# Moving two prefetched weight forms behind one subtraction, and naming the PSUM banks of a second pass, in a hybrid encoder layer

## The chip, the core and the metric

The kernel runs on one core of a Trainium2 chip. The metric is device time in microseconds (us), the median of several executions. The core has a matrix engine (TensorE, PE in the profile, with its weight loads listed apart as PEld), a vector engine (VectorE, DVE), a scalar engine (ScalarE, ACT), GpSimd (POOL) and a queue that issues DMAs (SyncE, SP). Products land in PSUM, which here is used as eight banks of 128 partitions x 512 float32. Everything else lives in SBUF.

## The reference

One layer of a bidirectional encoder on x of shape (1, 512, 1024), all float32. A token mixer (retention plus a gated spatial unit) comes first, and then the part that the change touches, a convolutional gated MLP with 2816 hidden columns per half:

```python
def _conv_gated_mlp(h, w_up, conv_w, conv_b, w_down):
    hid = h @ w_up                                   # (512, 1024) @ (1024, 5632)
    hid = depthwise_conv_of_width_3(hid) + conv_b    # along the sequence
    a, b = jnp.split(hid, 2, axis=-1)
    return (jax.nn.gelu(a) * b) @ w_down             # (512, 2816) @ (2816, 1024)

h2 = _rmsnorm(x, g_pre_ffn)
x = x + _rmsnorm(_conv_gated_mlp(h2, ...), g_post_ffn)
```

## The kernel before

**Arithmetic.** Every float32 operand is split into a high and a low part (line 85: `copy(hi, src)` on ACT, then `tensor_sub(lo, src, hi)` on DVE, which is line 87 in the profile), and each product is three matrix instructions: high by high, high by low, low by high. Two-by-two block products are done with seven block products in place of eight (Winograd's form of Strassen's scheme), so weights and activations are also needed as sums and differences, called forms.

**Up product.** The 44 weight blocks of the up product make 22 tiles of a (gate half, value half) pair. Tiles 4 to 19 are taken in eight *couples* (line 40). In a couple the first tile's two blocks go through class `Pair` as seven form products of 12 matrix instructions of 256 columns each, and the second tile's two blocks go through `up_block` as plain products of 48 each, so a couple has 7 x 12 + 2 x 48 = 180 matrix instructions. Their order (lines 1016 to 1020) is: `part1` (four products: with weight forms B11, B21, T1, T2), the first `up_block`, `part2` (the third product into bank 0, with T3), the first half of the second `up_block`, `part3` (products with T4 into bank 0 and B22 into bank 2), the second half of the second `up_block`.

In `part2` the product with T3 is copied out of bank 0 by ACT (line 700) and then subtracted from what stands in bank 2 by DVE (line 701). The first product of `part3` writes bank 0 again, so it needs the copy of line 700. The second writes bank 2, so it needs the subtraction of line 701; it is followed by the subtraction of line 713.

**Weights.** `units` (lines 94 to 118) lists all weight units in the order of their use: in a couple B11, B21, T1, T2, a block, T3, T4, B22, a block. A form has size 1, a block size 2. `w_get` (line 208) hands out the next unit and, before it does, makes later ones as long as the sizes of those made and not yet handed out, the one handed out included, stay within a limit: 9 for a form, 10 for a block. Making a unit (`w_form`, `w_block`, `w_down`) issues its DMA on SP, its sums, its high part on ACT and its low part on DVE. For T1 that is two sums on DVE (lines 166 and 167), one on GpSimd (line 168, which makes T2), and the split. T4 is one sum on GpSimd (line 170) and the split. The raw weights live in 4 buffers and the split ones in 9 slots; a slot is free again when the matrix engine is done with what was in it.

An engine runs its instructions in the order in which they stand in its queue. That order comes from the order of the lines, rearranged by a scheduler that works with modelled times; `tc.issue_after(ins)` ties every instruction of its block that runs on the engine of `ins` to a place behind `ins`.

**Down product.** It runs in two passes over the halves of the output columns. In each pass `products` is called for nine j with 42 matrix instructions each (seven products M1, M2, M3, M5, M6, M7, M4, in this order, of six each), every product into a bank of its own over all j; `add_whole` adds the rows that are not in pairs. Behind the last j of pass one the results are combined out of PSUM by ACT and DVE (`steps`, lines 1092 to 1098), and at the same time pass two starts to fill banks again. In pass two each product takes a bank from the pool (`m[n] = ps()`, line 1046) when j is 0, in the order in which the banks were let go.

Of the kernel before, what the change touches and what calls it, by code (L numbers as in the profile page):

```python
# [28 lines left out]
LOOK = 4  # L29
# [19 lines left out]
def tile_block(ctx: ExitStack, tc, xT, x, wall, par, cs, wsp, bsp, gpost, gpre, gffn, out):  # L49
# [7 lines left out]
    def nm(s):  # L57
        uid[0] += 1
        return f"{s}_{uid[0]}"

    def blk(dt=F32, n="blk", shape=(P, S)):
        return sb.tile(list(shape), dt, tag="blk", bufs=NBLK, name=nm(n))

    def tmp(n="tmp", shape=(P, S)):
        return sb.tile(list(shape), F32, tag="tmp", bufs=6, name=nm(n))
# [7 lines left out]
    def ps(shape=(P, S)):  # L73
        return pp.tile(list(shape), F32, tag="ps", name=nm("ps"))
# [4 lines left out]
    def copy(o, i):  # L79
        nc.scalar.activation(out=o, in_=i, func=AF.Copy)  # L80
# [13 lines left out]
    units = []  # L94
    i = 0
    while i < NW:
# [7 lines left out]
        elif i == UP0 + 2 * COUPLES[0][0]:  # L104
# [3 lines left out]
            i = UP0 + 2 * COUPLES[-1][1] + 2  # L108
# [10 lines left out]
    w_ready, w_pos, w_held, w_raw = {}, [0, 0], [0], {}  # L119
# [79 lines left out]
    def w_size(u):  # L199
        return 2 if u[0] in ("blk", "q", "t") else 1  # L200

    def w_next():
        u = units[w_pos[1]]
        w_ready[w_pos[1]] = w_unit(u)
        w_pos[1] += 1
        return w_size(u)

    def w_get(look=LOOK):

        i = w_pos[0]  # L210
        w_pos[0] += 1
        room = 2 * look + (2 if w_size(units[i]) == 2 else 0)
        n = sum(w_size(u) for u in units[i : w_pos[1]])
        while w_pos[1] < len(units) and (w_pos[1] <= i or n + w_size(units[w_pos[1]]) <= max(room, 9 if look == LOOK else 0)):
            n += w_next()
        return w_ready.pop(i)

# [50 lines left out]
    for k in range(KD):  # L268
        xt = load_x(k)
        xts.append(xt)  # L270
        if k:
            x_low(k, xt)
        if k == 2:
            copy(hold[:, 0:16], as32(xl[1])[:, 0:16])
        wh, wl = w_get(1 if k < 4 else LOOK)
        if k == 0:
            x_low(k, xt)
            for half in range(2):
                for a, b in ((wh, xh), (wl, xh), (wh, xl)):
                    for m in range(4 * half, 4 * half + 4):  # L280
                        nc.tensor.matmul(
                            qk[m], a[:, m * P : (m + 1) * P], b[0], start=a is wh and b is xh, stop=False
                        )
            continue
        if k > 1 and (k - 2) % 4 < 2:
            x_scaled(k - 2, xts[k - 2])
        for m in range(8):
            c = slice(m * P, (m + 1) * P)
            mm3(qk[m], wh[:, c], wl[:, c], xh[k], xl[k], False, k == KD - 1)

    T0, T1 = slice(0, 256), slice(256, 512)
# [53 lines left out]
    v = nc.vector  # L345
# [125 lines left out]
    def t_group():  # L471

        acc = [ps() for _ in range(NT)]
        for kp in range(4):
            wh, wl = w_get()
            for t in range(NT):
                c = slice(t * P, (t + 1) * P)
                for kk in range(2):
                    k = 2 * kp + kk
                    f = slice(kk * S, (kk + 1) * S)  # L480
                    nc.tensor.matmul(acc[t], xh[k][:, c], wh[:, f], start=k == 0, stop=False)  # L481
                    nc.tensor.matmul(acc[t], xh[k][:, c], wl[:, f], start=False, stop=False)  # L482
                    nc.tensor.matmul(acc[t], xl[k][:, c], wh[:, f], start=False, stop=k == KD - 1)  # L483
            yield acc
# [158 lines left out]
    def f_block(ah, al, n, between=None):  # L643

        wh, wl = w_get()
        o = ps()
        for k in range(n):
            if between and k == n // 2:
                between()
            c = slice(k * P, (k + 1) * P)  # L650
            mm3(o, wh[:, c], wl[:, c], ah[k], al[k], k == 0, k == n - 1)
        return o
# [4 lines left out]
    class Pair:  # L657
# [38 lines left out]

        def part2(self):
            c0, c1 = self.t
            o = self.product(0, self.s("S3"), False)
            copy(c1[:, T1], o)  # L700
            v.tensor_sub(c1[:, T1], self.b[2][:, T0], c1[:, T1])  # L701
            self.w = w_get(), w_get()

        def part3(self):
            c0, c1 = self.t
# [202 lines left out]
    def h2_sums(i):  # L908

        a0, b0, a1, b1 = h2r[0][i], h2r[0][i + 2], h2r[1][i], h2r[1][i + 2]  # L910
        v.tensor_sub(b1, a1, b1)
        v.tensor_sub(a1, a0, a1)
        v.tensor_sub(a0, b1, a0)
        v.tensor_add(b0, b0, a0)
        for n, t in zip(("S1", "S2", "S3", "S4"), (b1, a0, a1, b0)):
            h2_parts(n, i, t)

    def h2_block(w, o, q):
        wh, wl = w
        for k in range(KD):  # L920
            c = slice(k * P, (k + 1) * P)
            mm3(o[:, q], wh[:, c], wl[:, c], *h2(k, q), k == 0, k == KD - 1)

    def up_block(between=None):
        w, o = w_get(), ps()
        h2_block(w, o, T0)
        if between:
            between()
        h2_block(w, o, T1)
        return o  # L930
# [73 lines left out]
    def tile_done(i, o):  # L1004
        gated(*(conv(t, 2 * i + s_) for s_, t in enumerate(o)))
        if i < COUPLES[-1][1]:
            if i in (7, 11, 13, 17):
                down_forms(len(dforms))
        elif len(dforms) < EAGER:
            down_forms(len(dforms))  # L1010

    couples = dict(COUPLES)
    i = 0
    while i < NF:
        if i in couples:
            p = Pair(None, lambda: tmp("c"), h2, h2forms)
            p.part1()
            o = [up_block()]
            p.part2()
            o.append(up_block(p.part3))  # L1020
            tile_done(i, p.t)
            tile_done(i + 1, o)
            i += 2
        else:
            o = []
            for e in (2 * i, 2 * i + 1):
                o.append(early_o[e] if e < EARLY else up_block())
            if i < 2:
                h2_sums(i)
                w_next()  # L1030
            tile_done(i, o)
            i += 1
# [5 lines left out]
    M1, M2, M3, M5, M6, M7, M4, M8 = range(8)  # L1038
    whole = []

    def products(m, j, steps={}):
        for n, (unit, at, act) in enumerate(UNITS):
            if n in (0, 3):
                wh, wl = w_get()
            if j == 0:
                m[n] = ps()
            f = slice(at * 256, (at + 1) * 256)
            ah, al = dforms[j][act]
            for t in range(2):
                c = slice(t * P, (t + 1) * P)  # L1050
                o = m[n][:, t * 256 : (t + 1) * 256]
                for i, (a_, w_) in enumerate(((ah, wh), (ah, wl), (al, wh))):
                    nc.tensor.matmul(  # L1053
                        o, a_[:, c], w_[:, f], start=j == t == i == 0,
                        stop=j == DP - 1 and i == 2 and n not in (M2, M3, M4), skip_group_check=True,
                    )
            steps.get(n, lambda: None)()
# [18 lines left out]
    m = {}  # L1076
    m[M8] = ps()
    late = list(range(EAGER, DP))
    c11, c12, c21, c22 = c4 = [blk(n="c") for _ in range(4)]
    e1, e3, uu, yy = tmp("e1"), tmp("e3"), tmp("uu"), tmp("yy")  # L1080

    def after6():
        v.tensor_add(uu, m[M6], e1)
        v.tensor_sub(c12, m[M5], uu)
        v.tensor_add(c12, c12, e3)

    def after7():
        v.tensor_add(e1, m[M7], uu)
        v.tensor_sub(yy, m[M5], e1)  # L1089
        v.tensor_add(c22, c22, yy)  # L1090

    steps = {
        M1: lambda: copy(e1, m[M1]),
        M2: lambda: v.tensor_add(c11, m[M2], e1),
        M3: lambda: copy(e3, m[M3]),
        M6: after6, M7: after7,
        M4: lambda: v.tensor_add(c21, m[M4], e1),
    }
    for j in range(DP):
        if j < WHOLE:  # L1100
            whole.append(two_parts(gp[2 * DP + j]))
        if j % 2 and late:
            down_forms(late.pop(0))
        products(m, j, steps if j == DP - 1 else {})
        if j in (3, 5):
            w = w_get()
            for t in range(NT):
                add_whole(m, t, j // 2 - 1, w, j == 5)
            if j == 5:
                copy(c22, m[M8])  # L1110
# [12 lines left out]
        v.tensor_add(qn[t][:, 0:1], qn[t][:, 2:3], qn[t][:, 3:4])  # L1123


    m = {}
    e1, uu, xx, yy = (blk(n="e") for _ in range(4))

    def after6():
# [3 lines left out]
    def after7():  # L1133
        v.tensor_add(uu, m[M7], uu)
        v.tensor_sub(yy, m[M5], uu)

    steps = {M1: lambda: copy(e1, m[M1]), M6: after6, M7: after7}
    for j in range(DP):
        products(m, j, steps if j == DP - 1 else {})
        if 1 < j < 2 + NT:  # L1140
            first_share(j - 2)
    ww = [w_get(), w_get()]
    m[M8] = ps()

    def rows(t, sc, z, xt, some=(0, 1, 2)):

# [16 lines left out]
    for t in (0, 2, 1, 3):  # L1163
        last = t == NT - 1
# [152 lines left out]
```

## Time and profile before

| | us |
|---|---|
| runs, median (lowest to highest) | 829.89 (827.95 to 831.93) |
| the profiled execution's own time | 832.1 |
| its span, first to last instruction | 830.3 |
| PE busy, share of the span | 819.6, 99% |
| DVE busy | 659.3, 79% |
| ACT busy | 430.9, 52% |
| GpSimd busy | 104.4, 13% |

In the profiled execution the couples run from 520.8 to 683.8 us, the last plain blocks of the up product until 709.5 us, pass one of the down product until 765.2 us and pass two until 822 us. A row of the timeline gives the start, the duration, the engine, the line, the operation, the tiles written and read, the shape, and in brackets how long the engine had stood idle before and what ended that. A row of the table by stretches gives, for each engine, busy time and in brackets the number of instructions that lie in the stretch wholly or in part. Matrix instructions overlap in the records (one lasts 0.28 us and the next starts 0.11 to 0.12 us after it), so the distance of their starts tells the pace and not their busy time.

### The profile page before, as it was taken

To read this page: it belongs to the slowest core of one execution; us is meant where nothing else is said; L and a number is where in the kernel's file an instruction comes from. 1 tells how busy PE (TensorE), PEld (TensorE's weight loads), DVE (VectorE), ACT (ScalarE), POOL (GpSimd) and SP (SyncE) were. 2 spreads that over 40 slices of the span, in tenths; PEclk is the share of its full clock that TensorE was granted. 3 is DMA by queue.
4 is the path that set the end of the run, shared out by engine and by line. 5 is a ranking of instruction groups with operands and counts; after the bars stand their busy time and mean duration, and the time that the engine had idled before them with its cause. 6 is when DMAs were issued, how large, how long until landed. Compare 5 with 4: busy or idle time off the path is not lost. (4 is left out here: it accounts for less than half of the span.)

```text
span 830.3 us, 14356 instructions
## 1 busy us (share of the span) xinstructions
PE 819.6 (99%) x5728; PEld 760.9 (92%) x5728; DVE 659.3 (79%) x1076; ACT 430.9 (52%) x733; POOL 104.4 (13%) x108
## 2 busy tenths in 40 slices
PE   9999999999999999999999999999999999999996
PEld 7888888888899999999988899999999999999995
DVE  7489898877897777767765679679899789997956
ACT  6635445546665444444444456456566566644532
POOL 0010000102221111133221201111111100000002
PEclk9999999999999999999999999999999999999999
DMA  8733222213233333233459121333323341243344
GB/s 279 258 115 104 75 77 77 76 52 99 69 102 126 102 102 93 87 100 102 121 178 349 64 67 37 105 104 99 116 91 101 110 147 50 77 141 103 115 128 127
DMA packets 29251, 93.84 MB, mean 113 GB/s; under 512 B 3392, under 2 KB 4032, under 8 KB 29184
## 3 DMA queue, kind: packets, MB, share of 16 engines
q1 hardware_dynamic: 26784, 86.58, 32.6%
q0 software_dynamic: 1968, 6.03, 2.3%
q8 instruction: 45, 0.74, 0.4%
q10 hardware_dynamic: 432, 0.30, 0.1%
q14 instruction: 22, 0.18, 0.1%
HBM read 88.19 MB, written 4.72 MB: 112 GB/s over the span
## 5 line engine op out<-in xcount | busy, mean ns | idle before, releaser
L87 DVE TENSOR_TENSOR wl<-raw,wh 128x1024 fp32r<-128x1024 f32 (+1 forms) x93 | 109.4, 1186 | 50.8 <-PE ps L673 27.3
L80 ACT ACTIVATE wf<-raw 128x512 fp32r<-128x512 f32 x140 | 85.3, 626 | 102.8 <-PE ps L220 45.0
L87 DVE TENSOR_TENSOR wf<-raw,wf 128x512 fp32r<-128x512 f32 x140 | 109.2, 795 | 26.8 <-ACT wf L80 25.9
L220 PE MATMUL ps<-h2l,wh 128*128 128x256 f32 x448 | 124.6, 279 | 0.2 <-DVE h2l L892 0.2
L219 PE MATMUL ps<-h2h,wh 128*128 128x256 f32 x448 | 123.7, 278 | 0.0
L221 PE MATMUL ps<-h2h,wl 128*128 128x256 f32 x448 | 123.7, 277 | 0.0
L673 PE MATMUL ps<-sh,wf 128*128 128x256 f32 x640 | 120.2, 277 | 0.1
L80 ACT ACTIVATE wh<-raw 128x1024 fp32r<-128x1024 f32 (+2 forms) x95 | 93.0, 989 | 35.9 <-DMA raw<-wall 13.3
L673 PEld LDWEIGHTS ps<-sh,wf 128*128 128x128 f32 x640 | 101.3, 188 | 0.8 <-DVE c L701 0.3
L673 PE MATMUL ps<-sl,wf 128*128 128x256 f32 x320 | 89.1, 278 | 0.0
L220 PEld LDWEIGHTS ps<-h2l,wh 128*128 128x128 f32 x448 | 83.9, 187 | 0.7 <-DVE h2l L892 0.7
L219 PEld LDWEIGHTS ps<-h2h,wh 128*128 128x128 f32 x448 | 83.8, 188 | 0.3 <-ACT h2h L80 0.3
L221 PEld LDWEIGHTS ps<-h2h,wl 128*128 128x128 f32 x448 | 83.9, 188 | 0.0
L481 PE MATMUL ps<-wh,xh 128*128 128x512 f32 x192 | 75.0, 391 | 0.0
L482 PE MATMUL ps<-wl,xh 128*128 128x512 f32 x192 | 74.9, 390 | 0.0
L483 PE MATMUL ps<-wh,xl 128*128 128x512 f32 x192 | 74.8, 390 | 0.0
L168 POOL TENSOR_TENSOR raw<-raw,raw 128x512 f32<-128x512 f32 x20 | 35.1, 1755 | 239.9 <-DVE raw L166 212.5
L1053 PE MATMUL ps<-dh,fh 128*128 128x256 f32 x216 | 60.9, 282 | 0.3 <-DVE yy L1089 0.2
L1053 PE MATMUL ps<-dh,fl 128*128 128x256 f32 x216 | 60.9, 282 | 0.0
L673 PEld LDWEIGHTS ps<-sl,wf 128*128 128x128 f32 x320 | 60.0, 188 | 0.3
L1053 PE MATMUL ps<-dl,fh 128*128 128x256 f32 x216 | 60.3, 279 | 0.0
L673 PE MATMUL ps<-xh,wf 128*128 128x256 f32 x288 | 54.4, 279 | 0.0
(309 smaller groups left out, 2040.1 us busy)
## 6 DMA issues: line engine op xcount, KB each, us to landing
raw<-wall SPq DMA_DIRECT2D x145, 512.0 KB, 3.6
x<-x SPq DMA_DIRECT2D x22, 256.0 KB, 5.5
xT<-xT SPq DMA_DIRECT2D x8, 256.0 KB, 5.4
x<-x POOLq DMA_DIRECT2D x8, 256.0 KB, 2.4
xT<-xT POOLq DMA_DIRECT2D x4, 256.0 KB, 3.8
out<-zs SPq DMA_DIRECT2D x3, 256.0 KB, 3.3
cs<-cs SPq DMA_DIRECT2D x2, 256.0 KB, 4.0
gpm<-gpost POOLq DMA_DIRECT2D x2, 256.0 KB, 3.8
```

Of the source, the lines that this page charges most:

```text
L80: nc.scalar.activation(out=o, in_=i, func=AF.Copy)
L87: nc.vector.tensor_sub(lo, src, as32(hi))
L168: nc.gpsimd.tensor_tensor(out=w_raw["T2"], in0=w_raw["T1"], in1=w_raw["B22"], op=ALU.add)
L219: nc.tensor.matmul(o, ah, bh, start=start, stop=False)
L220: nc.tensor.matmul(o, ah, bl, start=False, stop=False)
L221: nc.tensor.matmul(o, al, bh, start=False, stop=stop)
L481: nc.tensor.matmul(acc[t], xh[k][:, c], wh[:, f], start=k == 0, stop=False)
L482: nc.tensor.matmul(acc[t], xh[k][:, c], wl[:, f], start=False, stop=False)
L483: nc.tensor.matmul(acc[t], xl[k][:, c], wh[:, f], start=False, stop=k == KD - 1)
L673: nc.tensor.matmul(o, w_[:, c], a_, start=first and k == n == 0, stop=k == 3 and n == 2, skip_group_check=True,)
L1053: nc.tensor.matmul(o, a_[:, c], w_[:, f], start=j == t == i == 0, stop=j == DP - 1 and i == 2 and n not in (M2, M3, M4), skip_group_check= ...
```

## The change

Three edits.

1. `w_get` and `up_block` take `most`, an upper bound on the limit. The first `up_block` of a couple asks with 9 in place of 10, and the product with T3 in `part2` asks with 7 in place of 9. With these bounds the making of T1 and T2 of the next couple does not fit before the subtraction of line 701; it falls to the next `w_get`, which in a couple stands inside `tc.issue_after(last.ins)`, where `last` is that subtraction. So the DVE instructions that make these forms, and the low part of the block that follows them, stand behind the subtraction in DVE's queue. In the other uses of `Pair` nothing changes.
2. Pass two of the down product no longer takes banks from the pool. A table names, for each of its products, the bank of pass one that it writes: M1 that of M8, M2 that of M1, M3 that of M2, M5 that of M3, M6 its own, M7 that of M5, M4 that of M7, M8 that of M4.
3. The steps that combine pass one's results are put in another order, with the same operations: behind M6 only `uu`; behind M7 `e1`, `yy` and the difference for `c12`; behind M4 `c21` and the two remaining additions for `c12` and `c22`.

```diff
-    def w_get(look=LOOK):
+    def w_get(look=LOOK, most=99):
...
-        while w_pos[1] < len(units) and (w_pos[1] <= i or n + w_size(units[w_pos[1]]) <= max(room, 9 if look == LOOK else 0)):
+        while w_pos[1] < len(units) and (w_pos[1] <= i or n + w_size(units[w_pos[1]]) <= min(most, max(room, 9 if look == LOOK else 0))):
             n += w_next()
...
         def part2(self):
             c0, c1 = self.t
-            o = self.product(0, self.s("S3"), False)
+            couple = self.scale is None
+            o = self.product(0, self.s("S3"), False, w_get(most=7 if couple else 99))
             copy(c1[:, T1], o)
-            v.tensor_sub(c1[:, T1], self.b[2][:, T0], c1[:, T1])
-            self.w = w_get(), w_get()
+            last = v.tensor_sub(c1[:, T1], self.b[2][:, T0], c1[:, T1])
+            if couple:
+                with tc.issue_after(last.ins):
+                    self.w = w_get(), w_get()
+            else:
+                self.w = w_get(), w_get()
...
-    def up_block(between=None):
-        w, o = w_get(), ps()
+    def up_block(between=None, most=99):
+        w, o = w_get(most=most), ps()
...
-            o = [up_block()]
+            o = [up_block(most=9)]
...
-            if j == 0:
+            if j == 0 and n not in m:
                 m[n] = ps()
...
-    def after6():
-        v.tensor_add(uu, m[M6], e1)
-        v.tensor_sub(c12, m[M5], uu)
-        v.tensor_add(c12, c12, e3)
-
     def after7():
         v.tensor_add(e1, m[M7], uu)
         v.tensor_sub(yy, m[M5], e1)
+        v.tensor_sub(c12, m[M5], uu)
+
+    def after4():
+        v.tensor_add(c21, m[M4], e1)
+        v.tensor_add(c12, c12, e3)
         v.tensor_add(c22, c22, yy)
...
-        M6: after6, M7: after7,
-        M4: lambda: v.tensor_add(c21, m[M4], e1),
+        M6: lambda: v.tensor_add(uu, m[M6], e1), M7: after7, M4: after4,
...
-    m = {}
+    m = {n: m[o] for n, o in ((M1, M8), (M2, M1), (M3, M2), (M5, M3), (M6, M6), (M7, M5), (M4, M7), (M8, M4))}
...
-    m[M8] = ps()
```

## The prediction

> **What bounds the kernel now.** I read the shares of busy time first, then the stretches of the second half, then the timeline around the places where the matrix engine's starts are uneven.
>
> ```profile
> PE 819.6 (99%) x5728; PEld 760.9 (92%) x5728; DVE 659.3 (79%) x1076; ACT 430.9 (52%) x733; POOL 104.4 (13%) x108
> ```
>
> PE is busy 99% of the span. So time can come only from the pace of its instructions, or from waits so short that they hardly show in a share. The table by stretches (one couple per stretch, then the last plain blocks, then the two down passes; columns PE, PEld, DVE, ACT, POOL, clock, DMA share, GB/s) tells the pace.
>
> ```profile
> 216.82:262.60 45.78, 45.78 (x386) 45.57 (x385) 40.88 (x62) 29.93 (x55) 10.22 (x8) 1.00 0.32 104
> ...
> 541.17:561.57 20.40, 20.40 (x182) 20.40 (x181) 15.63 (x25) 11.20 (x20) 2.93 (x2) 1.00 0.35 105
> ...
> 602.37:622.77 20.40, 20.40 (x182) 20.40 (x181) 20.07 (x32) 12.39 (x22) 2.95 (x2) 1.00 0.28 85
> 622.77:643.83 21.06, 20.99 (x182) 20.78 (x181) 20.83 (x32) 12.88 (x24) 2.93 (x2) 1.00 0.32 101
> 643.83:665.23 21.40, 21.40 (x182) 21.40 (x181) 17.22 (x27) 12.64 (x22) 2.93 (x2) 1.00 0.39 120
> 665.23:683.78 18.55, 18.55 (x158) 18.55 (x157) 16.35 (x27) 10.78 (x18) 0.00 (x0) 1.00 0.48 144
> 683.78:709.46 25.68, 25.68 (x219) 25.68 (x217) 25.28 (x45) 14.98 (x24) 0.00 (x0) 1.00 0.17 53
> 709.46:765.20 55.74, 55.74 (x476) 55.74 (x475) 48.56 (x79) 29.27 (x41) 0.59 (x1) 1.00 0.33 105
> 765.20:822.00 56.80, 56.49 (x477) 56.00 (x475) 43.49 (x75) 22.85 (x42) 4.24 (x6) 1.00 0.36 108
> ```
>
> A couple is 180 matrix instructions (the counts hold two or three more that reach in). The four from 541.17 to 622.77 (first and last shown) take 20.40 us each, 113.3 ns an instruction. At 643.83 the same couple takes 21.40 us, 118.9 ns, with PE busy throughout and the granted clock at 1.00 in both. So there are two paces, 5.6 ns apart, and the slower one can last without any wait: 384 instructions from 216.82 on went at 119.2 ns. The change of pace falls into the couple from 622.77:
>
> ```profile
> 637.50 0.28 PE L220 MATMUL ps<-h2l,wh 128*128 128x256 f32 x1
> 637.62 0.28 PE L221 MATMUL ps<-h2h,wl 128*128 128x256 f32 x1
> 637.74 0.34 PE L673 MATMUL ps<-h2h,wf 128*128 128x256 f32 x1
> 637.91 0.28 PE L673 MATMUL ps<-h2l,wf 128*128 128x256 f32 x1
> ...
> 639.10 0.28 PE L673 MATMUL ps<-h2h,wf 128*128 128x256 f32 x1
> 639.45 0.39 PE L673 MATMUL ps<-sh,wf 128*128 128x256 f32 x1
> ```
>
> Starts are 0.11 to 0.12 us apart, then 0.17 where `part3` begins (637.74 to 637.91), then 0.35 before its second product. After that the fast pace does not return before the end. What held the two products, from the timelines of ACT, POOL and DVE:
>
> ```profile
> 636.73 0.63 ACT L80 ACTIVATE wf<-raw 128x512 fp32r<-128x512 f32 x1 [1.84 <-DVE raw L166]
> 637.26 0.37 ACT L80 ACTIVATE c<-ps 128x256 f32<-128x256 f32 x1
> 636.86 1.64 POOL L168 TENSOR_TENSOR raw<-raw,raw 128x512 f32<-128x512 f32 x1 [16.79 <-DVE raw L166]
> 635.34 0.69 DVE L87 TENSOR_TENSOR fl<-gp,fh 128x512 fp32r<-128x512 f32 x1
> 635.94 0.69 DVE L166 TENSOR_TENSOR raw<-raw 128x512 f32<-128x512 f32 x1
> 636.66 0.69 DVE L167 TENSOR_TENSOR raw<-raw,raw 128x512 f32<-128x512 f32 x1
> 637.39 1.67 DVE L87 TENSOR_TENSOR wf<-raw,wf 128x512 fp32r<-128x512 f32 x1
> 638.98 0.41 DVE L701 TENSOR_TENSOR c<-ps,c 128x256 f32<-128x256 f32 x1
> ```
>
> The copy of line 700 (637.26) stood behind the high part of T1, which waited for the sum of line 166; the first product of `part3` waited for that copy. The subtraction of line 701 (638.98) stood behind both sums and T1's low part; the second product waited for it. All that is late because DVE comes out of `down_forms` with no idle time (20.83 busy of 21.06).
>
> **Edit 1, what it removes.** With T1 behind line 701, the copy has nothing of T1 ahead of it: bank 0 is complete 24 instructions before 637.74 (2.7 us), near 635.2 with the last one's 0.28, and ACT is idle for 1.84 us before 636.73, so it ends near 635.6. Line 701 follows the `fl` of 635.34, at about 635.95, and ends near 636.35, against a need at 639.1. Both waits go. Direct: this couple needs 21.06 instead of 20.40, but of the 0.66 us some 0.2 is the slow pace of its last 36 instructions (36 x 5.6 ns). Then the pace: if it stays fast because nothing disturbed it, 336 instructions from 643.83 to 683.78 gain 39.95 - 336 x 0.1133 = 1.88 us, and 216 from 683.78 to 709.46 gain 25.68 - 24.47 = 1.21 us. Together 0.66 + 1.88 + 1.21 = 3.75 us up to the down product.
>
> **What edit 1 moves.** Per couple: two DVE sums, two DVE low parts, two ACT high parts, one POOL sum. Their DMAs were issued with B11, whose place is unchanged, and SP's order is the same. In the couple of 622.77 they only swap with line 701: DVE does 0.69 + 0.69, the blocked 1.67, then T2's low part, as before and 0.4 us earlier. In couples with a free DVE they really come later:
>
> ```profile
> 552.14 1.16 ACT L80 ACTIVATE wf<-raw 128x512 fp32r<-128x512 f32 x2 [3.90 <-PE ps L220]
> 554.03 0.42 DVE L701 TENSOR_TENSOR c<-ps,c 128x256 f32<-128x256 f32 x1
> 557.75 1.23 DVE L87 TENSOR_TENSOR wl<-raw,wh 128x1024 fp32r<-128x1024 f32 x1 [3.29 <-PE ps L673]
> 559.63 0.42 DVE L713 TENSOR_TENSOR c<-ps,c 128x256 f32<-128x256 f32 x1
> ```
>
> From line 701's end at 554.4: the first sum 0.7, POOL 1.65, T2's high part 0.6, its low part 0.7, so T2 is whole near 558.1. The next couple's product with T1 starts 24 instructions after 561.57, at 564.3; 6 us of cover. DVE had 3.29 us idle there, ahead of the block's low part at 557.75; that hides it. ACT's wait for POOL puts its next copies, and line 713, back by about 1 us; they are needed only for banks of the couple after. I take 0, with 0 to 0.7 us per couple as bounds (the upper: the 0.66 us excess of the couple of 622.77, the one late couple that the trace shows).
>
> The row at 637.39 took 1.67 instead of 0.69 us while POOL's sum ran from 636.86 to 638.50. The Trainium skill, "SBUF — State Buffer", section "Who interferes with whom", says that a vector instruction with two SBUF inputs and a GpSimd instruction that reads SBUF exclude each other for the whole instruction. It speaks against the change: T1's low part now lies under line 168 in every couple, where the free couples had it behind. By it these pay 1.0 us of DVE each, as the row has it; the 3.29 us idle cover that too, so the sum is the same by rule and by row, and only the slower rival feeds on it.
>
> **What is late next.** DVE is nearly full from 683.78 on (25.28 of 25.68), and one weight part of the down product comes only just in time: the low part of the fourth set of summed weights (`w_down`, form "t"; 1024 wide, counted from the first), ahead of the product that reads it in the fourth j:
>
> ```profile
> 724.91 1.23 DVE L87 TENSOR_TENSOR dl<-raw,dh 128x1024 fp32r<-128x1024 f32 x1
> 726.53 0.28 PE L1053 MATMUL ps<-dl,fh 128*128 128x256 f32 x1
> ```
>
> It ends 0.4 to 0.5 us ahead of its use. PE would arrive 3.75 us sooner, DVE only as much sooner as its own start (about 0.66 + 1.88 = 2.5 us at 683.78). So a new wait of 3.75 - 2.5 - 0.45 = 0.8 us; bounds 0 (other work of DVE is reordered) and 1.25 (no margin). Left: 2.95 us.
>
> **Edits 2 and 3.**
>
> ```profile
> 768.70 0.28 PE L1053 MATMUL ps<-dh,fl 128*128 128x256 f32 x1
> 769.09 0.36 PE L1053 MATMUL ps<-dh,fh 128*128 128x256 f32 x1
> ...
> 769.99 0.28 PE L1053 MATMUL ps<-dl,fa 128*128 128x256 f32 x1
> 770.47 0.39 PE L1053 MATMUL ps<-dh,fh 128*128 128x256 f32 x1 [0.19 <-DVE yy L1089]
> ```
>
> ```profile
> 764.99 0.68 DVE L1083 TENSOR_TENSOR uu<-ps,e 128x512 f32<-128x512 f32 x1
> 765.93 0.68 DVE L1084 TENSOR_TENSOR c<-ps,uu 128x512 f32<-128x512 f32 x1
> 766.53 1.22 DVE L87 TENSOR_TENSOR dl<-raw,dh 128x1024 fp32r<-128x1024 f32 x1
> 767.66 0.69 DVE L1085 TENSOR_TENSOR c<-c,e 128x512 f32<-128x512 f32 x1
> 768.26 0.69 DVE L1088 TENSOR_TENSOR e<-ps,uu 128x512 f32<-128x512 f32 x1
> 769.73 0.69 DVE L1089 TENSOR_TENSOR yy<-ps,e 128x512 f32<-128x512 f32 x1
> ```
>
> M7 of pass two (769.09) came when line 1088 was done with a bank, M4 (770.47) when line 1089 was. Against a start distance of 0.12 the two cost about 0.27 and 0.36 us, and 0.2 with the longer starts behind them: 0.8 in all. After the change M7 takes M5's bank, free after `e1`, `yy` and the `c12` difference. These start at 765.9 and last 3 x 0.6 us; with one weight split (1.13 us) between them they end at 768.9, against a need at 768.8. M4's bank is free earlier. (The split is the row at 766.53, to the next start.) Without a split in between nothing is left of the wait, with two 1.2. I take 0.1, so a gain of 0.7, bounds -0.4 and 0.8. The additions for `c12` and `c22` move back by about 2 us; they feed the squares on ACT, busy 22.85 of 56.80 in this pass, which costs nothing.
>
> **Sum.** 832.1, the profiled execution's own time, less 2.95, less 0.7: 828.4. The runs' median of 829.89 lies 2.2 below that execution and the lowest 4.1 below; if faster runs are those that met the wait of 637 later or not at all, they gain less, and if they are only shifted, 826.2 follows. I take the middle, 827.3, and shift all cases below by the same 1.1.
>
> **Rivals.**
>
> A. The fast pace lives on through both down passes. They hold 474 instructions each, at 55.74 / 474 = 117.6 ns; at 113.3 each gains 2.0 us. 827.3 - 4.1 = 823.2. For it: the fast pace held through four couples, across forms and blocks. Against: no row shows line 1053 at 113 ns, the tight row at 724.91 gives a new disturbance.
>
> B. The pace does not hang on the wait; it falls back for another reason, or the next disturbance comes at once. Then only waits go: 0.66 - 0.2 + 0.7 = 1.2, and no new wait at 724.91. 829.8, no change to be measured. For it: the slow pace at 216.82 without waits. Beside it: the Trainium skill, "TensorE: Matmul & The Clock Gate", section "Back-to-back issue gap", gives one distance for 256 columns, 262 cycles or 109 ns, with no second pace; by that rule the removed wait would be worth its own length alone. Against: both paces stand here for the same lines and shapes.
>
> C. Slower. In the couples with `down_forms` DVE has no room (20.07 of 20.40). There the moved forms with POOL's blocking push line 713 and the next couple's line 690 by over 1 us, and PE meets a wait in the first such couple, near 577. It decides once DVE is later than 2 us at line 713. Price: the wait, 0.66 us in each of four such couples, 2.6, and the slow pace 60 us sooner, 540 x 5.6 ns = 3.0; and none of edit 1's 2.95 gain. 832.1 + 5.6 - 0.7 - 1.1 = 835.9. Against: in the one couple that was late, the work behind 701 keeps its order.
>
> **Chances.** Forecast 0.42, A 0.24, B 0.20, C 0.14. Faster or slower means by over 0.5% of 829.89, about what this measurement can tell: under 825.7 or over 834.0. A is faster, and the better part of the forecast's low end adds some: 0.32. C nearly all slower: 0.13. The rest, 0.55. The forecast's own range is 825.5 to 829.5; from A's 823.2, less the same 0.8 us of unknowns, to B's with the worst bounds and the edge of C: 822.4 to 833.5.
>
> **What would show it.** No 0.35 us gap before the second product of `part3`; line 701 right behind the copy of line 700 in each couple, lines 166 to 168 behind it; every couple at 20.4 us; 216 plain instructions in about 24.5 us. A new gap near the fourth j of pass one. Line 1053 at 117.6 or 113.3 ns decides between forecast and A. One distance over 0.45 us at the start of pass two would refute the 0.7. A couple over 20.6 us before 622 would make the prediction wrong, toward C.

## The result, and the profile after

The changed kernel took 833.89 us (median; 832.07 to 834.46), the kernel before 830.02 us in the same measurement. The ratio is 1.0036, 95% interval 1.0021 to 1.0050: a little slower, by less than the 0.5% named in the prediction but by more than the measurement's uncertainty, and 0.4 us above the predicted range. (The ratio is the measurement's own and not the quotient of the two medians, which differ by 3.9 us, 0.47%.) The profiled execution has 834.26 us and a span of 832.5, against 832.1 and 830.3.

From the changed kernel's page, the shares of busy time:

```profile
PE 821.5 (99%) x5728; PEld 763.4 (92%) x5728; DVE 665.5 (80%) x1076; ACT 430.8 (52%) x733; POOL 105.0 (13%) x108
```

The number of instructions is the same on each engine. DVE is busy 6.2 us longer, PE 1.9 us. The table by stretches of the changed kernel, one couple per row (columns as in the prediction), says where PE's time goes:

```profile
561.68:582.08 20.40, 20.40 (x182) 20.40 (x181) 19.96 (x31) 12.73 (x23) 2.93 (x2) 1.00 0.33 104
582.08:604.01 21.93, 21.46 (x183) 21.26 (x181) 19.01 (x28) 12.11 (x21) 2.94 (x2) 1.00 0.30 99
604.01:625.41 21.40, 21.40 (x183) 21.40 (x181) 20.96 (x33) 13.33 (x24) 2.95 (x2) 1.00 0.31 100
625.41:646.81 21.40, 21.40 (x183) 21.40 (x181) 20.96 (x33) 13.35 (x25) 2.94 (x2) 1.00 0.32 98
```

The fast pace of 113.3 ns ends not near 638 but in the couple from 582.08, two couples sooner. That couple costs 1.53 us more than the 20.40 it had, the next 1.00 more, the one from 625.41 0.34 more than the 21.06 it had: 2.87 us together. PE reaches the down product at 712.43 instead of 709.46. The second part of the kernel gives back 0.5 us in pass two and 0.3 us behind the last matrix instruction (why the last is open), which leaves the 2.2 us of the span.

PE's timeline in the changed kernel, at the place where the pace changes, and at `part3` of the couple from 625.41, the place in the program where it changed before:

```profile
586.05 0.28 PE L673 MATMUL ps<-sh,wf 128*128 128x256 f32 x1
586.79 0.39 PE L673 MATMUL ps<-sh,wf 128*128 128x256 f32 x1 [0.47 <-ACT c L80]
587.02 0.28 PE L673 MATMUL ps<-sl,wf 128*128 128x256 f32 x1
...
641.10 0.28 PE L673 MATMUL ps<-h2h,wf 128*128 128x256 f32 x1
641.22 0.28 PE L673 MATMUL ps<-h2l,wf 128*128 128x256 f32 x1
...
642.41 0.28 PE L673 MATMUL ps<-h2h,wf 128*128 128x256 f32 x1
642.53 0.28 PE L673 MATMUL ps<-sh,wf 128*128 128x256 f32 x1
```

In `part3` (641.10, and its second product at 642.53) the starts are now even, 0.12 us apart: both waits are gone, as predicted. In their place stands one distance of 0.74 us, 36 instructions into the couple: the fourth product (with T2) writes bank 0, and waits for the copy of line 688, which takes the first product out of that bank. ACT's timeline of the changed kernel leads up to that copy (the row at 586.37), with POOL's and DVE's rows behind:

```profile
578.49 0.63 ACT L80 ACTIVATE wf<-raw 128x512 fp32r<-128x512 f32 x1 [1.24 <-POOL raw L168]
579.03 1.05 ACT L80 ACTIVATE wh<-raw 128x1024 fp32r<-128x1024 f32 x1
...
582.67 0.82 ACT L967 ACTIVATE cv<-c,part 128x512 f32<-128x512 f32 x1 [0.95 <-DVE c L718]
...
585.85 0.62 ACT L80 ACTIVATE wf<-raw 128x512 fp32r<-128x512 f32 x1
586.37 0.37 ACT L80 ACTIVATE c<-ps 128x256 f32<-128x256 f32 x1
```

```profile
576.81 1.64 POOL L168 TENSOR_TENSOR raw<-raw,raw 128x512 f32<-128x512 f32 x1 [17.02 <-DVE raw L166]
```

```profile
575.58 0.41 DVE L702 TENSOR_TENSOR c<-ps,c 128x256 f32<-128x256 f32 x1
575.91 0.67 DVE L166 TENSOR_TENSOR raw<-raw 128x512 f32<-128x512 f32 x1
577.28 2.56 DVE L87 TENSOR_TENSOR wf<-raw,wf 128x512 fp32r<-128x512 f32 x2
580.11 2.19 DVE L87 TENSOR_TENSOR wl<-raw,wh 128x1024 fp32r<-128x1024 f32 x1 [0.26 <-ACT wh L80]
582.22 0.41 DVE L718 TENSOR_TENSOR c<-ps,c 128x256 f32<-128x256 f32 x1
```

The answering rows of the kernel before (its line 713 is line 718 now, its line 701 line 702), DVE first, then ACT. In its profile the couples begin 0.11 us sooner (520.77 against 520.88), so 0.11 us of each difference below is only this offset:

```profile
573.84 0.69 DVE L166 TENSOR_TENSOR raw<-raw 128x512 f32<-128x512 f32 x1
...
578.15 2.19 DVE L87 TENSOR_TENSOR wl<-raw,wh 128x1024 fp32r<-128x1024 f32 x1 [0.26 <-ACT wh L80]
...
580.92 0.41 DVE L713 TENSOR_TENSOR c<-ps,c 128x256 f32<-128x256 f32 x1
```

```profile
581.37 0.82 ACT L962 ACTIVATE cv<-c,part 128x512 f32<-128x512 f32 x1 [1.28 <-DVE c L713]
...
584.98 0.37 ACT L80 ACTIVATE c<-ps 128x256 f32<-128x256 f32 x1
```

Read from its start, it is one chain over four engines. T1's sum comes 2.07 us later (575.91 for 573.84), as it now stands behind line 702. POOL's sum for T2 follows (576.81 to 578.45), then ACT's high part of T2 (578.49), then, queued behind it on ACT, the high part of a whole block (579.03), then on DVE that block's low part (580.11 for 578.15), and behind that line 718 (582.22 for 580.92). The convolution of the value half of the couple's first tile reads what line 718 writes, so ACT starts it at 582.67 instead of 581.37. ACT then has six pieces to do (582.67 to 585.85) before the copy of line 688 of the *next* couple, in its order of issue: the copy ends at 586.74, where it ended at 585.35 before. PE wanted to write the bank at 586.16. It is 0.63 us late (0.746 less 0.113), and the pace is slow from the next instructions on: 0.63 + 0.11 for the second long distance + 143 instructions at 5.5 ns more are the 1.53 us of this couple.

Behind the two later couples with `down_forms` there is no such wait, as the slow pace gives ACT and DVE 1.0 us more in each couple: there the same copy ends about 1.0 us before it is needed (628.70 for 629.69, 650.12 for 651.09).

At the start of pass two, PE's and DVE's rows of the changed kernel:

```profile
771.73 0.28 PE L1058 MATMUL ps<-dh,fl 128*128 128x256 f32 x1
771.98 0.39 PE L1058 MATMUL ps<-dh,fh 128*128 128x256 f32 x1
```

```profile
771.25 0.68 DVE L1090 TENSOR_TENSOR c<-ps,uu 128x512 f32<-128x512 f32 x1
```

The wait of M4 is gone and that of M7 is 0.14 us (0.257 less 0.118), until the `c12` difference (771.25) lets its bank go. In pass one the fourth set of summed weights is late by 0.05 us only, since PE came no sooner.

### The profile page after: what moved, and what is told of

It is laid out like the page before. It is cut to its first block, busy times and chain, and to the rows that moved or that the text cites. A ratio compares the mean times of both kernels' runs of the same rounds, so it can differ in the third digit from the quotient of the medians.

```text
span 832.5 us, 14368 instructions
## 1 busy us (share of the span) xinstructions
PE 821.5 (99%) x5728; PEld 763.4 (92%) x5728; DVE 665.5 (80%) x1076; ACT 430.8 (52%) x733; POOL 105.0 (13%) x108
## 4 chain that ended last, share of the span: by engine, by line
PE 89%; DVE 5%; issue 2%; ACT 2%; POOL 1%; DMA 0%; POOLq 0%; ACTq 0%; DVEq 0%
PE ps L673 22%; PE ps L220 12%; PE ps L219 12%; PE ps L221 12%; PE ps L1058 11%; PE ps L482 5%; PE ps L481 5%; PE ps L483 5%; PE ps L1075 2%; PE ps L751 1%; PE ps L828 1%; PE ps L827 1%; PE ps L826 1%; POOL qr L845 1%; PE ps L281 1%
## 5 line engine op out<-in xcount | busy, mean ns | idle before, releaser
L87 DVE TENSOR_TENSOR wl<-raw,wh 128x1024 fp32r<-128x1024 f32 (+1 forms) x93 | 113.4, 1229 | 38.6 <-PE ps L673 20.0
L87 DVE TENSOR_TENSOR wf<-raw,wf 128x512 fp32r<-128x512 f32 x140 | 113.4, 824 | 22.3 <-ACT wf L80 21.1
```

The lines of the kernel that those rows point to most:

```text
L87: nc.vector.tensor_sub(lo, src, as32(hi))
```

## The experiments

Each ratio below is against the kernel before in the same measurement; its median was 831.61 us beside `edit1_alone`, `pass2_alone`, `one_couple` and `wait_early`, 831.50 beside the two `sums_early` kernels, `convs_behind` and `after_t2_dve`, and 830.46 beside the four `spread` kernels. The diffs show the lines that matter, and their comments are notes for the reader.

Theory P: the whole loss is edit 1's, through the chain above. Against it: the loss is in edits 2 and 3; or the pace turns slow for a reason of its own and the wait at 586.79 only happens to stand there.

**Edit 1 alone, edits 2 and 3 alone.** Kernel `edit1_alone` has the first edit of the diff and nothing else, `pass2_alone` the other two.

> Edit 1 in all couples, without the named banks and the new order of the steps of the down product. Theory P (the pace hangs on waits: the first wait of the matrix engine in the couples turns the pace from 113.3 to 118.9 ns and it stays so): the changed kernel's 0.75 us wait near 587 us, ahead of the product with T2, is there, every couple behind it at 21.4 us; the two waits of before at the start of the second down pass (0.8 us) are there too; 833.0 to 835.0. Theory R (the named banks or the new order of the steps cost the time): about 830.0, and couples at 20.4 us up to 622. Theory Q (waits count for their own length alone): 830.4.

> Edits 2 and 3 alone; the couples are those of before. P and Q: the couples as before, the wait near 637 too; the waits at the start of the second pass fall from 0.8 to about 0.3 us; 829.5, no difference that can be told. R: 833 or more.

Edit 1 alone: 834.58 us, ratio 1.0038 (1.0024 to 1.0051); the same wait, 754 ns between two starts at 586.14, the slow pace behind it, and in pass two the waits for the two banks again (distances of 247 and 471 ns). Edits 2 and 3 alone: 831.77, 1.0001 (0.9992 to 1.0010); the waits near 638 are there, and in pass two two distances of 219 and 227 ns are left of four of 394, 194, 473 and 227, which is 0.6 us less. So the loss is edit 1's, and edits 2 and 3 do what they say, for an amount that the medians don't resolve.

**Taking one link out of the chain.** Kernel `after_t2_dve` is the changed kernel with T2's sum on VectorE in the couples; `sums_early` is edit 1 with the three sums back ahead of the subtraction and only the splits behind it.

```diff
-            nc.gpsimd.tensor_tensor(out=w_raw["T2"], in0=w_raw["T1"], in1=w_raw["B22"], op=ALU.add)
+            (nc.vector if i >= UP0 else nc.gpsimd).tensor_tensor(out=w_raw["T2"], in0=w_raw["T1"], in1=w_raw["B22"], op=ALU.add)
```

```diff
             o = [up_block(most=9 if p.behind else 99)]
+            if units[w_pos[1]][0] == "T1":
+                w_sums()          # the sums of lines 166 to 168
+                w_raw["sums"] = 1  # w_form then makes no sums of its own
```

> The changed kernel with T2's sum (line 168) of the couples on VectorE in place of GpSimd: 0.6 us more of DVE in a couple, but no sum of GpSimd that blocks the low part of T1 and no wait for it. Worked out from the changed kernel's rows, T2 is split 0.8 us sooner, against a wait of 0.75 us near 587. P: the wait shrinks to under 0.1 us; if it is over 0.03 us the pace turns slow all the same, 833; if it is none, 829 to 830. If GpSimd is not the cause: 834.5.

> Edit 1 in all couples, but the three sums that make T1, T3 and T2 stay ahead of line 701, behind the first plain block as before; only the splits of T1 and T2 stand behind line 701. No edits 2 and 3. Theory P (any wait in the couples, even 0.04 us, turns the pace slow for the rest of the up product): POOL's sum is over before the splits are due in most couples, so line 713 is no later than before, the copy of line 688 is in time, and no couple has a wait; fast pace up to the down product, 3.75 us under a run of before with its wait, 827 to 828.5; 4 us less again if the fast pace goes on in the down passes. Theory Q (waits count for their own length): 831.2, 0.4 under before.

`after_t2_dve`: 830.37 us, 0.9990 (0.9980 to 1.0001). DVE in the couple that was late:

```profile
576.18 0.68 DVE L168 TENSOR_TENSOR raw<-raw,raw 128x512 f32<-128x512 f32 x1
578.52 2.25 DVE L87 TENSOR_TENSOR wl<-raw,wh 128x1024 fp32r<-128x1024 f32 x1 [0.26 <-ACT wh L80]
580.70 0.41 DVE L718 TENSOR_TENSOR c<-ps,c 128x256 f32<-128x256 f32 x1
```

0.68 us on DVE instead of 1.64 on POOL, and no blocked subtraction: line 718 is back at 580.70, and the wait at 587 does not occur. `sums_early` (831.05, 0.9996, 0.9984 to 1.0009) has none there either. So the chain runs through POOL's late sum; whether its length or the subtraction that it blocks weighs more, these two kernels do not separate. (In the changed kernel DVE was done with the blocked rows at 579.84 and then still waited 0.26 us for ACT.) Both kernels meet their first wait later, at the copy of line 688 near 647 (starts 331 and 192 ns apart), where two couples with `down_forms` have followed each other. In `after_t2_dve` the pace turns slow there; in the profiled execution of `sums_early` (829.54) it stays fast. Neither median reaches what was expected without a wait (829 to 830, and 827 to 828.5).

With edits 2 and 3 added to the early sums:

> The kernel sums_early with edits 2 and 3. P: as sums_early, and 0.5 us less for the waits at the start of the second down pass; 826.5 to 828. Q: 830.7.

It took 830.65 us, 0.9990 (0.9979 to 1.0001), where 826.5 to 828 was expected: the same first wait, a distance of 197 ns at 646.89, and the slow pace behind it.

**Moving the six pieces away from ahead of the copy.** Kernel `convs_behind` is the changed kernel with the convolutions and the gating of a couple issued behind the next couple's `part1`.

```diff
             p.part1()
+            catch_up()        # tile_done of the couple before
             o = [up_block(most=9)]
...
-            tile_done(i, p.t)
-            tile_done(i + 1, o)
+            left += [(i, p.t), (i + 1, o)]
```

> The changed kernel, with the convolution and gating of a couple's tiles issued behind the first four products of the next couple in place of ahead of them. Theory P1 (the wait near 587 comes because the copy of line 688 stands behind convolutions on ScalarE that wait for DVE): the copy follows its product at once, the wait near 587 is gone, and the pace stays at 113.3 ns unless another wait comes; 828 to 830. Theory P2 (the fourth product waits for T2 itself, which comes late): the wait stays, 834.

It took 840.95 us, 1.0123 (1.0105 to 1.0142). The convolutions are gone from ahead of the copy, but ACT now reaches the split of T4 first and stands there 3.16 us for POOL's sum of line 170, and the copy behind it is 2.8 us late. The expectation missed: what matters is all that stands ahead of the copy in ACT's queue, not the convolutions as such.

**Does the pace hang on the wait?** `wait_early` is the kernel before with six more copies on ACT ahead of that of line 688 in the second couple (into a tile that is written again later); `one_couple` is the kernel before with edit 1 in the couple of tiles 14 and 15 alone (its diff is shown against the changed kernel).

```diff
             o = self.product(0, self.x(0, T0), True)
+            for _ in range(self.extra):   # 6 where i == 6, else 0
+                copy(c1[:, T0], o)
             copy(c0[:, T0], o)
```

```diff
-            couple = self.scale is None
+            couple = self.behind          # i == 14
```

> The kernel before with six more copies of 128x256 out of bank 0 on ScalarE in the couple of tiles 6 and 7, ahead of the copy that the fourth product of that couple waits for (they write what is overwritten later; nothing of the computation is left out). Six times 0.37 us less 1.6 us of cover make one wait of about 0.6 us near 545 us. P: the pace turns slow there, some 815 instructions 5.6 ns each sooner than before: 0.6 + 4.6, 834 to 836. Q: 830.6.

> Edit 1 in one couple alone, the one of tiles 14 and 15, in which the kernel before has its waits (638 to 639.5 us); no edits 2 and 3. P: no wait in any couple, 113.3 ns up to the down product near 705.7 us in the profile, a gain of 3.75 us on a run that had the wait; 826 to 828 in the median, and the runs closer together. Q: the two waits go, 0.4 us, and the pace turns slow near 640 anyway; 829.6.

`wait_early`: 834.36 us, 1.0030 (1.0012 to 1.0047). Its PE rows and its couples:

```profile
544.72 0.28 PE L220 MATMUL ps<-h2l,wh 128*128 128x256 f32 x1
545.73 0.39 PE L674 MATMUL ps<-sh,wf 128*128 128x256 f32 x1 [0.74 <-ACT c L80]
```

```profile
539.50:560.80 21.30, 20.56 (x175) 20.37 (x174) 16.15 (x24) 12.63 (x26) 3.01 (x2) 1.00 0.31 91
560.80:582.20 21.40, 21.40 (x182) 21.40 (x181) 20.06 (x33) 13.29 (x24) 2.93 (x2) 1.00 0.32 96
```

One made wait, of 0.90 us where 0.6 was meant, and couples that took 20.40 in the kernel before take 21.40 from there on. From the start of the couples to the down product it is 193.78 us (519.10 to 712.88) against 188.69, 5.1 us more; the median shows 2.8 of them, and the ten runs lie far apart (830.07 to 837.14). `one_couple`: 830.83, 0.9989 (0.9980 to 0.9997), where 826 to 828 was expected. The wait near 638 is gone, but the next couple's copy of line 688 is some 0.04 us late, and the pace turns slow there:

```profile
646.58 0.43 PE L674 MATMUL ps<-sh,wf 128*128 128x256 f32 x2
646.85 0.28 PE L674 MATMUL ps<-sl,wf 128*128 128x256 f32 x1
```

**Taking away what makes VectorE late.** A further theory, Q: VectorE is late near 638 and 647 because tiles 11 and 13 put `down_forms` into two couples in a row. Kernel `spread` is the kernel before with one line changed, `spread_after` the changed kernel with the same line, `spread_sums_pass2` adds it to the early sums with edits 2 and 3, `spread_t2_dve` to `after_t2_dve`.

```diff
-            if i in (7, 11, 13, 17):
+            if i in (5, 9, 13, 17):
```

> The kernel before, with the gated forms of the down product (`down_forms`, line 1007) made behind tiles 5, 9, 13 and 17 in place of 7, 11, 13 and 17, so that no two couples in a row carry them; nothing else is changed. Theory Q: VectorE is late around 640 because two couples in a row (those from 602 and 623 us) carry these forms. With one couple of rest between them no start distance over 0.15 us is left in the couples, all couples take 20.4 us, the fast pace of 113.3 ns holds to the end of the up product near 705.7, and the 0.7 us wait for the low part of the fourth set of summed weights comes near 723.5: the whole is 3.75 - 0.7 = 3 us shorter, 827.5 to 829.5. Theory R: the slow pace comes at its own time, with or without a wait: at most 1 us is gained.

> The changed kernel with the forms of the down product behind tiles 5, 9, 13 and 17. Theory P (the sum of T2 on GpSimd and T1's split, now behind the subtraction, need only one couple with these forms to be late): the copy of line 688 is late in the couple behind the first such one, near 566, by 0.5 to 1 us, and the pace is slow from there: 834 to 836. Theory Q (only two couples in a row are too much): no wait in the couples, 827 to 829.5.

> The changed kernel with the sums that make T1, T3 and T2 back ahead of line 701 (the splits stay behind it), and with the forms of the down product behind tiles 5, 9, 13 and 17. If the wait near 647 that was left with the early sums came from two couples in a row with these forms: no start distance over 0.15 us in the couples, fast pace to 705.7, then the 0.7 us wait near 723.5, pass two with two short waits: 827 to 828.5, faster than both kernels. If the slow pace comes at its own time: 830 to 831.

> The changed kernel with the sum that makes T2 on VectorE in the couples, and with the forms of the down product behind tiles 5, 9, 13 and 17. If two couples in a row with these forms were what was left: no wait in the couples, fast pace to 705.7, 827 to 828.5. If VectorE is late behind a single such couple already: a wait of 0.2 to 0.5 us in a copy of line 688 and 830 to 832.

`spread`: 828.34 us (826.78 to 829.64) against 830.46, ratio 0.9972 (0.9961 to 0.9982). One of its last couples and its plain blocks by stretches, and its PE in pass one:

```profile
622.55:642.96 20.41, 20.41 (x183) 20.41 (x182) 20.08 (x32) 12.40 (x22) 2.96 (x2) 1.00 0.28 88
681.80:706.30 24.50, 24.50 (x218) 24.50 (x217) 24.24 (x44) 14.28 (x22) 0.00 (x0) 1.00 0.18 52
```

```profile
722.47 0.28 PE L1053 MATMUL ps<-dh,fh 128*128 128x256 f32 x1
723.24 0.39 PE L1053 MATMUL ps<-dl,fh 128*128 128x256 f32 x1 [0.48 <-DVE dl L87]
```

No wait in any couple, and 113.3 ns up to 705.5. From the start of the couples (520.56, before 520.77) to the down product it is 184.95 us, before 188.69: 3.7 us less. Then the low part of the fourth set of summed weights is late, by 0.65 us (0.763 less 0.118).

`spread_after`: 834.04, 1.0039 (1.0025 to 1.0053). With edit 1, one couple with `down_forms` is enough to be late, as expected:

```profile
561.65:582.81 21.16, 20.67 (x182) 20.48 (x181) 18.62 (x27) 11.72 (x20) 2.94 (x2) 1.00 0.32 101
582.81:603.21 20.40, 20.40 (x182) 20.40 (x181) 19.95 (x31) 12.75 (x23) 2.94 (x2) 1.00 0.31 104
603.21:625.17 21.96, 21.47 (x182) 21.27 (x181) 19.02 (x28) 12.13 (x21) 2.94 (x2) 1.00 0.33 99
```

It waits at 566.4 and 607.9 (starts 765 and 767 ns apart). Behind the first the pace stayed fast (20.40), which was not expected; behind the second it did not.

`spread_sums_pass2`: 828.22, 0.9970 (0.9960 to 0.9980), no wait in the couples, one of 0.7 us near 723.8 and none over 0.02 us in pass two. `spread_t2_dve`: 829.39, 0.9988 (0.9978 to 0.9998); no wait in the couples, but 1.7 us at 724.25, and a time between the two that were expected. All three are faster than both kernels; the kernel before with one line changed (`spread`) is as fast as any, and edit 1 is not needed for it. For 638, theory Q holds; for edit 1, `spread_after` shows that a single such couple is too much.

## Why the prediction was wrong

**The step that failed** is the cost of what edit 1 moves, taken as 0 with "6 us of cover". Cover was counted for the forms themselves, up to the product that reads T1, and for DVE. Of ACT's wait for POOL the prediction said that the copies and line 713 move back "by about 1 us; they are needed only for banks of the couple after". Line 713 did move by 1.3 us. But its result is also read by a convolution on ACT, and behind that convolution, in ACT's queue, stands the copy of line 688, needed 4.08 us into the next couple. From line 713's end to that copy's end are 4.1 us of ACT work, so line 713 has to be done about when the couple ends. Before, it was done 0.6 us ahead of that. Nor did idle time of DVE give 6 us: the chain starts at line 702 in every couple and takes about 6.65 us to line 718 (533.74 to 540.40 in a couple where DVE had stood idle, 575.58 to 582.22 here). In the first of these the copy ends at 544.91 for a need at 545.36, so even there only 0.45 us was left, and behind `down_forms` line 702 is some 1.0 us later in its couple. The price was 0.63 us of waiting where the upper bound was 0.7; what that bound did not hold is that the wait brings the slow pace forward, so that the 3.75 us were never gained and 2.9 us were lost in the couples. The sign named for it, a couple over 20.6 us before 622, is the 21.93 from 582.08.

**The size of the gain was right, but not of this edit.** Removing the waits near 638 was put at 3.75 us up to the down product; `spread`, which removes them otherwise, gained 3.7. It hung on the condition that nothing else disturbs PE: in `one_couple`, where edit 1 stands in the couple of those waits alone, the next couple's copy was 0.04 us late and the gain was gone. The new wait of 0.8 us in pass one came with 0.65 us there and 0.70 in `sums_early`. In the changed kernel PE came 2.97 us later to that place instead of 3.75 sooner.

**Edits 2 and 3**: 0.7 us predicted, 0.57 measured in the changed kernel (four long distances, 0.82 us over the regular ones, became two with 0.25), with the one weight split in between that the prediction assumed.

**The blocking.** T1's low part does lie under POOL's sum in the couples now: 2.56 us for two rows of 577.28 that take 1.28 when nothing blocks. The rule of the Trainium skill, "SBUF — State Buffer", section "Who interferes with whom", that the prediction weighed (a vector instruction with two SBUF inputs and a GpSimd instruction that reads SBUF exclude each other) agrees with the trace. In the free couples PE did not wait for it, but in the couple from 561.68 DVE had little idle time (19.96 busy of 20.40).

**Rivals.** A (the fast pace lives on in the down product) falls by `sums_early`, which enters it fast and without a wait; its rows go from 113 to 118 ns at the first instruction of line 1067 (line 1053 before):

```profile
705.64 0.28 PE L225 MATMUL ps<-h2h,wl 128*128 128x256 f32 x1
705.75 0.28 PE L1067 MATMUL ps<-dh,fa 128*128 128x256 f32 x1
705.87 0.28 PE L1067 MATMUL ps<-dl,fa 128*128 128x256 f32 x1
```

B has two halves. That the pace falls back for another reason than the wait is refuted by `wait_early` and `spread`. That the next disturbance comes at once is what `one_couple` showed for the waits near 638: with those two waits alone removed, the pace turned slow at 646.85 and the gain was 0.1%. The one distance of 109 ns that the prediction set beside B is kept neither in the up product nor in the down product: the starts there are 113.3 to 118.9 ns apart. C was what happened, with a chance of 0.14: the moved forms with POOL's blocking push line 713, and PE meets a wait in the couples with `down_forms`. It was priced at 835.9 with the place at 577, four waits and 540 slow instructions; it was 587, one wait of 0.63 us and some 425 slow instructions (587.0 to 637.6 at 0.119). C's own threshold, 2 us at line 713, was too high, since it looked at the bank of that line and not at ACT's queue behind it.

## What to carry to other kernels

When work is moved back on one engine, follow each result that becomes late through *every* queue behind its readers, to the first instruction of the bounding engine that stands there: here the way from a sum to the wait led over four engines, and the slack was 0.6 us where the direct reader had 6. Before reordering a crowded stretch, look at what crowds it: to move a bundle of other work to other couples removed the same waits, at the price of one wait of 0.65 us later. And a short wait can cost more than its length where it also changes the pace behind it.

## What the runs showed of the hardware

**The pace.** In the couples the matrix engine keeps 113.3 ns for as long as it meets no wait (three kernels out of three without a wait were fast to the end of the up product), and a wait as short as 0.04 us can turn it to 118.9 for all that follows there. It does not always: behind 0.65 us in `spread_after` (566.4) and 0.08 us in `sums_early` (647.2) it stayed fast, while 0.08 us at nearly the same place in `sums_early_pass2` turned it slow.

The change also goes the other way. Ahead of the couples each of the fourteen kernels has two short disturbances in a run of plain products (lines 219 to 221 here): a few transposes of line 886, and then one distance of 0.2 us between two starts near 478, and of 0.31 us near 487. Between the two stand 71 products; here they are in the kernel before and then in `spread`, whose engines have the same instructions in the same order up to 540 us, from the first product behind the long distance to the next transpose:

```profile
478.44 0.28 PE L220 MATMUL ps<-h2l,wh 128*128 128x256 f32 x1
...
486.88 0.49 PE L886 MATMUL ps<-ident,xn 128*128 128x128 f32 x3
```

```profile
478.58 0.28 PE L220 MATMUL ps<-h2l,wh 128*128 128x256 f32 x1
...
486.65 0.82 PE L886 MATMUL ps<-ident,xn 128*128 128x128 f32 x6
```

That is 118.8 ns an instruction against 113.6. Eight of the fourteen profiles have the slow pace there (118.8 to 119.0), six the fast one; behind the second disturbance all fourteen are fast, 113.3 ns. So a disturbance can turn the pace either way, and in the up product no profile changes it without one. That it turned slow at 586.79 in the changed kernel is thus no matter of the wait's length alone. What decides it, and what the two paces are, is open; the granted clock is 1.00 in both. That nine of the twelve runs of `sums_early` lie between 830.6 and 831.9 us and three between 826.9 and 829.5 would fit such a choice; this was not shown. In the down product the distance is 117.6 to 117.8 ns whatever went before, but for some 42 us of `spread_after` (728 to 770), where it is 117.0.

**Half the clock after a long wait.** PE in `convs_behind`, around its first wait, and the stretch behind it (the clock is the column before the last two):

```profile
585.26 0.28 PE L673 MATMUL ps<-sh,wf 128*128 128x256 f32 x1
588.17 0.38 PE L673 MATMUL ps<-sh,wf 128*128 128x256 f32 x1 [2.63 <-ACT c L80]
...
590.09 0.41 PE L219 MATMUL ps<-h2h,wh 128*128 128x256 f32 x1
590.31 0.41 PE L220 MATMUL ps<-h2l,wh 128*128 128x256 f32 x1
```

```profile
589.23:592.50 3.27, 3.27 (x18) 3.27 (x17) 2.97 (x5) 3.04 (x6) 0.00 (x0) 0.50 0.58 177
```

PE stood idle for 2.63 us, went on at full clock for 1 us, then ran at half the clock (213 ns apart) for 3.3 us, and afterwards again at the fast pace. A distance of 2.83 us between two starts at 656.6 was followed by such a stretch too, one of 1.77 us at 632.4 was not. By the trace's own record of the granted clock the two stretches at half the clock last 3.41 us each (from 589.17 and from 657.43), and they begin 68.27 us apart, 20 times 3.413. That would fit fixed windows of this length, counted on whatever the kernel does, which would also say why the clock fell only 1 us after work went on; from three waits it is not shown. The Trainium skill, "TensorE: Matmul & The Clock Gate", part 1, names an idle window of about 3.4 us for the fall to half the clock; in this trace 2.6 us of idleness, and 2.9 us between two starts, were enough.
